# An S5, attention and DeltaNet kernel on one core: whole-row rotations in S5, one sum moved to GpSimd, small copies moved to ScalarE

## The chip, the cores and the metric

The kernel runs on one core of one Trainium2 chip. Its time is the device time of one execution in microseconds; three runs of the kernel before gave 1975.92, 1976.27 and 1977.36, median 1976.27. Besides, one execution was profiled, and all durations below come from that one.

## The reference

Two layers of a hybrid backbone run over 128 context tokens and 512 latent tokens, 640 in all, with 1024 features each. Layer 0 mixes with two heads side by side, layer 1 with a gated DeltaNet; a squared-ReLU MLP follows each, and every sub-layer has its norm and its modulation by a condition. The change lies in the mixer of layer 0:

```
def _s5_scan(u, lam_re, lam_im, log_dt, b_re, b_im, c_re, c_im, x0):
    lam_bar = jnp.exp(lam * jnp.exp(log_dt)[:, None])
    b_bar = ((lam_bar - 1) / lam)[..., None] * lax.complex(b_re, b_im)
    bu = jnp.einsum('gnp,blgp->blgn', b_bar, u)
    bu = bu.at[:, 0].add(lam_bar * x0)
    _, xs = lax.associative_scan(comb, (a, bu), axis=1)     # x_t = lam_bar x_(t-1) + bu_t, complex
    y = jnp.einsum('gpn,blgn->blgp', c_mat, xs).real
    return y, xs[:, -1]

def _even_mixer_latent(h, ck, cv, x0_re, x0_im, w_in, w_out, s5p, rpb):
    u, q, k, v = _even_split(h, w_in)
    a_out, _, _ = _s5_mixer(u, x0_re, x0_im, *s5p)          # forward and backward scan
    b_out = _neighbourhood_attention(q, k, v, ck, cv, rpb)  # 8 heads, windows of 8 x 16 and the cache
    return jnp.concatenate([a_out, b_out], axis=-1) @ w_out
```

S5 has 32 groups with 64 complex states each and two directions.

## The kernel before

All of layer 0 and 1 stays on the core; weights are streamed by SyncE's DMA queue. A weight block is loaded as fp32 (`raw`), split into a high part on ScalarE (`whi`, L194) and a low part on GpSimd (`wlo`, L196), and every product runs as three TensorE passes (L205 to L207).

The mixer of layer 0 first projects u, then q, k and v of four head pairs; between these products stand the steps of S5. S5 works in four blocks of eight groups, each with two directions `d`: eight units. Eight time steps are folded into one, so that a group has 65 folded steps of the latent stream and 17 of the context (82 columns; one of each holds the start state). A unit (`s5_unit`, L769) does this:

- VectorE builds the folded input weights `bp` (L785 to L787, two products and a sum of 1024 elements per partition). TensorE transposes them (L792) and multiplies them with the inputs (L809), and ScalarE copies the result to `W` (L811).
- VectorE builds the folded output weights `ct` (L798 to L800, two products and a sum of 1152 elements).
- The complex recurrence is turned into a real one: `W` is rotated by a table of angles, scanned with a real decay (L844, L846), and rotated back. Real and imaginary parts lie in partitions 0 to 63 and 64 to 127, so a rotation needs a swapped copy of its source: two DMAs on SyncE (L825, L826). Then `rotate` (L828) multiplies the source by the cosines (L832) and the swapped copy by the sines with its sign (L833), and adds them (L834).
- The final state is copied out (L851). A tile of start states goes into `W` by a copy of eight elements (L814).

`s5_tables` (L870) makes the cosines and sines of a block: GpSimd copies the first nine columns (L875), VectorE doubles them up to 65 (L864 to L867), and three DMAs bring them to the other halves of the partitions and to the other direction (L878, L879). The table has 65 columns; the 17 context columns use its first 17, so each product over 82 columns is two instructions, over 8 x 65 = 520 and over 8 x 17 = 136 elements.

`s5_taps` forms the taps (`kk`, L910, L912) from `ct`; `s5_back` multiplies states and inputs out (L938 to L942) and applies the gelu. Attention (`attention`, L966) runs in blocks of 128 queries: scores (L993), softmax, transposes of the probabilities (L1011), their copies from PSUM (`pT`, L1013 on ScalarE, L1015 on VectorE), products with the values (L1019). Beside it run the modulation products of later sub-layers (`mod_half`, L271), whose rows are copied from PSUM by VectorE (`mrow`, L287).

The order on every engine is set when the program is built: a planner with a cost model of its own places each instruction of the whole program, by priorities that the code gives; each engine then runs its list in that order. Tiles come from rings: `BUFS` (L1850) says how many buffers a tag has, and the writer of a buffer waits for the last reader of the tile that had it before.

Of the kernel before, what the change touches and what calls it, by code (L numbers as in the profile page):

```python
# [148 lines left out]
class Build:  # L149
# [94 lines left out]
    def mod_setup(self):  # L244
# [15 lines left out]
        self.raws = {}  # L260

# [9 lines left out]
    def mod_half(self, l, nb, kh, P, tag="pc", row=None, dst=None):  # L271
# [11 lines left out]
        if kh == 1:  # L283
            rp, rt, rb = row or (self.sp, "nf", 3)
            row = rp.tile([128, 256], F32, name="mrow", tag=rt, bufs=rb)
            if dst is None:
                nc.vector.tensor_copy(row, p[:, :256])  # L287
            else:
                nc.scalar.activation(row, p[:, :256], AF.Copy)
# [479 lines left out]
    def s5_unit(self, b, d, P, U, tb):  # L769
# [30 lines left out]
        V.tensor_tensor(ct, ct, t2, op=SU)  # L800
# [13 lines left out]
        V.tensor_copy(W[:, :, ex:ex + 1], self.s5x0[:, ps].unsqueeze(2))  # L814
        V.memset(W[:, :, ez:ez + 1], 0.0)

        def segs(t):
            so = t[:, :, 0:65], t[:, :, 65:82]
            return so
        def tab(t):  # L820
            return (t, t[:, :, 0:17]) if d == 0 else (t[:, :, ::-1], t[:, :, 16::-1])
# [6 lines left out]
        def rotate(src, op, out):  # L828
            sw = swap(src, "sw")
            m = self.tl([128, 8, 82], "s5g")  # L830
            for so, c_, s_, w_, m_ in zip(segs(src), tab(tb[:, 0]), tab(tb[:, 1]), segs(sw), segs(m)):
                V.tensor_tensor(m_, so, c_, op=M)  # L832
                V.scalar_tensor_tensor(w_, w_, sgn, s_, op0=M, op1=M)  # L833
            V.tensor_tensor(out, m, sw, op=op)  # L834
# [16 lines left out]
        V.tensor_copy(self.s5fin[:, p0:p0 + 8].unsqueeze(2), Sv[:, :, fin:fin + 1])  # L851
# [18 lines left out]
    def s5_tables(self, b, P):  # L870

        nc = self.nc
        t = [self.tl([128, 2, 8, 65], "rt") for d in range(2)]
        w = self.PA.tile([128, 512], F32, name="rt1")
        nc.gpsimd.tensor_copy(t[0][:, :, :, 0:9], self.s5e[:, :, 8 * b:8 * b + 8])  # L875
        self.turns(t[0], 8, 64, w)
        for r in range(2):
            nc.sync.dma_start(out=t[1][64 * r:64 * r + 64], in_=t[0][64:128])  # L878
        nc.sync.dma_start(out=t[0][64:128], in_=t[0][0:64])  # L879
# [86 lines left out]
    def attention(self, hp, qkv, ab, P):  # L966
# [16 lines left out]
        def block(qs, keys, vts, kind):  # L983
# [24 lines left out]
            for hh in range(2):  # L1008
# [3 lines left out]
                if hp < 2 or hh:  # L1012
                    nc.scalar.activation(pT[hh][:, :n], p[:, :n], AF.Copy)  # L1013
                else:
                    V.tensor_copy(pT[hh][:, :n], p[:, :n])  # L1015
# [834 lines left out]
    BUFS = dict(s5g=6, s5s=6, s5o=3, bp=1, bpt=1, ct=4, rt=2, vts=2,  # L1850
                cv=3, khT=2, ktok=2, vtok=2, cb=2, otok=2, osq=1)

    def run(self, stop=None):
        nc, A, tc = self.nc, self.A, self.tc
        with contextlib.ExitStack() as es:
# [35 lines left out]
            with contextlib.ExitStack() as ph:  # L1891
# [11 lines left out]
                with phase("l0") as P:  # L1903
# [5 lines left out]
                    steps, qkv = self.even_s5(hn, P)  # L1909
                    rx.close()  # L1910
# [17 lines left out]
                    for m in mods:  # L1928
                        self.mod_half(*m, P, tag="pb")
                    with tc.high_priority(offset=1000):  # L1930
# [67 lines left out]
```

## Time and profile before

| | us |
|---|---|
| median of three runs | 1976.27 |
| the profiled execution | 1976.35 |
| its span, first to last instruction | 1974.1 |
| TensorE busy | 1799.6 (91%) |
| VectorE busy | 1290.8 (65%) |
| ScalarE busy | 869.5 (44%) |
| GpSimd busy | 760.8 (39%) |

The profile's page gives shares over the whole span; the parts of the program have different limits, so the views below are cut to stretches. Times in a trace are counted from the first instruction. The letters PE, PEld, DVE, ACT, POOL and SPq stand for TensorE's matmuls, its weight loads, VectorE, ScalarE, GpSimd and SyncE's issues. A busy matmul time is a modelled one, since matmuls overlap.

### The profile page before, as it was taken

Reading aid. Unit: us, or ns where it says so; the run is one execution under the profiler, and the core shown is the slowest. Engines: PE = TensorE matmul, PEld = TensorE weight load, DVE = VectorE, ACT = ScalarE, POOL = GpSimd, SP = SyncE. Lnnn points to the kernel's source line nnn. Section 1 sums busy time; section 2 is a strip of 40 time slices with the busy share of each in tenths; the row PEclk is TensorE's granted clock in tenths of the full one; section 3 lists DMA queues with packets and bytes.
Section 4 is the critical chain, followed back from the end, with each engine's and each line's share of the span. In section 5 each row is a group of like instructions: output and inputs, shape, how many; then the busy total and the mean of one; then the engine's idle time right before and its main releaser. Section 6 shows DMA issues by size and latency. Waiting matters only on the chain. (4 is left out here: it accounts for less than half of the span.)

```text
span 1974.1 us, 35755 instructions
## 1 busy us (share of the span) xinstructions
PE 1799.6 (91%) x13556; PEld 1698.3 (86%) x13556; DVE 1290.8 (65%) x2825; ACT 869.5 (44%) x1928; POOL 760.8 (39%) x609
## 2 busy tenths in 40 slices
PE   5889889998999999998877889889989899999998
PEld 3789677988999999998877788787878899999997
DVE  8999777369264544548589988774667927364553
ACT  4333356344244353536454455344324425344362
POOL 2622101442343433453455555522235334343451
PEclk9999999998999999998998999898989999999999
DMA  8446886524332222332576478758834122222231
GB/s 319 131 112 169 239 246 228 195 106 140 124 112 84 76 86 75 135 123 78 158 207 196 117 197 238 222 166 267 279 131 149 54 97 76 86 76 86 76 96 54
DMA packets 206985, 286.61 MB, mean 145 GB/s; under 512 B 54879, under 2 KB 138237, under 8 KB 206813
## 3 DMA queue, kind: packets, MB, share of 16 engines
q1 hardware_dynamic: 206812, 284.33, 45.6%
q8 instruction: 107, 1.75, 0.4%
q14 instruction: 66, 0.53, 0.1%
HBM read 228.87 MB, written 46.82 MB: 140 GB/s over the span
## 5 line engine op out<-in xcount | busy, mean ns | idle before, releaser
L196 POOL TENSOR_TENSOR wlo<-raw,whi 128x1024 fp32r<-128x1024 f32 (+1 forms) x153 | 360.8, 2361 | 512.6 <-ACT whi L194 466.6
L194 ACT ACTIVATE whi<-raw 128x1024 fp32r<-128x1024 f32 (+1 forms) x153 | 153.2, 1002 | 324.5 <-PE pg L206 146.6
L207 PE MATMUL pg<-hidh,wlo 128*128 128x320 f32 (+2 forms) x576 | 178.8, 311 | 0.5 <-POOL wlo L196 0.5
L205 PE MATMUL pg<-hidh,whi 128*128 128x320 f32 (+2 forms) x576 | 179.0, 311 | 0.0
L206 PE MATMUL pg<-hidl,whi 128*128 128x320 f32 (+2 forms) x576 | 178.9, 311 | 0.0
L205 PE MATMUL pg<-h10h,whi 128*128 128x320 f32 x472 | 158.9, 337 | 17.5 <-DVE cb L1722 6.5
L422 DVE SCALAR_TENSOR_TENSOR x<-pg,mod,x 128x128 f32<-128x128 f32 (+2 forms) x132 | 53.7, 436 | 179.5 <-PE pg L207 179.5
L206 PE MATMUL pg<-h10l,whi 128*128 128x320 f32 x472 | 155.9, 330 | 0.0
L207 PE MATMUL pg<-h10h,wlo 128*128 128x320 f32 x472 | 155.3, 329 | 0.0
L205 PE MATMUL pa<-hidh,whi 128*128 128x320 f32 x448 | 138.0, 310 | 0.5 <-ACT whi L194 0.5
L207 PE MATMUL pa<-hidh,wlo 128*128 128x320 f32 x448 | 138.4, 309 | 0.0
L206 PE MATMUL pa<-hidl,whi 128*128 128x320 f32 x448 | 138.2, 309 | 0.0
L422 DVE SCALAR_TENSOR_TENSOR x<-pa,mod,x 128x128 f32<-128x128 f32 (+2 forms) x108 | 43.8, 435 | 136.8 <-PE pa L207 136.8
L507 POOL TENSOR_TENSOR wq<-S,wq 128x512 fp32r<-128x512 f32 x52 | 71.3, 1371 | 114.4 <-ACT wq L506 114.4
L205 PEld LDWEIGHTS pg<-h10h,whi 128*128 128x128 f32 x472 | 95.9, 203 | 21.4 <-DVE cb L1722 7.2
L207 PEld LDWEIGHTS pg<-hidh,wlo 128*128 128x128 f32 x576 | 108.2, 188 | 1.6 <-POOL wlo L196 1.0
L205 PEld LDWEIGHTS pg<-hidh,whi 128*128 128x128 f32 x576 | 108.3, 188 | 0.9 <-issue 0.8
L206 PEld LDWEIGHTS pg<-hidl,whi 128*128 128x128 f32 x576 | 108.2, 188 | 0.4 <-DVE hidl L568 0.3
L1322 DVE SCALAR_TENSOR_TENSOR cv<-cb,cw,cv 128x642 f32<-128x642 f32 x90 | 94.6, 1052 | 9.8 <-ACT cv L1319 8.9
L206 PEld LDWEIGHTS pg<-h10l,whi 128*128 128x128 f32 x472 | 95.9, 203 | 0.6 <-issue 0.4
L207 PEld LDWEIGHTS pg<-h10h,wlo 128*128 128x128 f32 x472 | 95.6, 203 | 0.2
L205 PEld LDWEIGHTS pa<-hidh,whi 128*128 128x128 f32 x448 | 83.9, 188 | 2.0 <-ACT whi L194 1.2
(742 smaller groups left out, 5754.2 us busy)
## 6 DMA issues: line engine op xcount, KB each, us to landing
raw<-in_wff SPq DMA_DIRECT2D x104, 512.0 KB
mraw<-in_wmod SPq DMA_DIRECT2D x96, 512.0 KB
raw<-in_wino SPq DMA_DIRECT2D x33, 512.0 KB
rawx<-in_wff SPq DMA_DIRECT2D x24, 512.0 KB
raw<-in_wine SPq DMA_DIRECT2D x16, 512.0 KB
cka<-pd SPq DMA_DIRECT2D x28, 256.0 KB
ckb<-pd SPq DMA_DIRECT2D x28, 256.0 KB
s5g<-s5g SPq DMA_DIRECT2D x32, 164.0 KB
```

Source lines behind the costliest of these rows:

```text
L194: nc.scalar.activation(hi[:, :kt], raw[:, :kt], AF.Copy)
L196: (nc.vector if self.lov and self.nw % self.lov else nc.gpsimd).tensor_tensor(lo[:, :kt], raw[:, :kt], hi[:, :kt], op=ALU.subtract)
L205: nc.tensor.matmul(p[:, :n], hi[:, k], xh[:, s], start=(k == 0), stop=False)
L206: nc.tensor.matmul(p[:, :n], hi[:, k], xl[:, s], start=False, stop=False)
L207: nc.tensor.matmul(p[:, :n], lo[:, k], xh[:, s], start=False, stop=(k == kt - 1))
L422: nc.vector.scalar_tensor_tensor(x[m][:, s], p[:, ls], g, x[m][:, s], op0=ALU.mult, op1=ALU.add)
L507: (V if j % 2 else nc.gpsimd).tensor_tensor(t[:, 4:8], src, t[:, 0:4], op=SU)
L1322: V.scalar_tensor_tensor(cv, cb[m][:, t:t + 642], cw[:, t:t + 1], cv, op0=M, op1=AD)
```

## The change

Five edits in the mixer of layer 0. The tables of angles get 82 columns (17 of them copies, made by GpSimd), so that `rotate` needs one instruction per product; the first product now overwrites its source, and the tile `m` goes, with one buffer of the ring `s5g`. The sum that ends `ct` goes from VectorE to GpSimd. The copies of start and final states, of all `pT`, and of `mrow` while the mixer runs go from VectorE to ScalarE.

```
@@ mod_half
-            if dst is None:
+            if dst is None and not self.rowact:
                 nc.vector.tensor_copy(row, p[:, :256])
             else:
                 nc.scalar.activation(row, p[:, :256], AF.Copy)
@@ s5_unit
-        V.tensor_tensor(ct, ct, t2, op=SU)
+        nc.gpsimd.tensor_tensor(ct, ct, t2, op=SU)
...
-        V.tensor_copy(W[:, :, ex:ex + 1], self.s5x0[:, ps].unsqueeze(2))
+        nc.scalar.activation(W[:, :, ex:ex + 1], self.s5x0[:, ps].unsqueeze(2), AF.Copy)
...
-        def segs(t):
-            so = t[:, :, 0:65], t[:, :, 65:82]
-            return so
-        def tab(t):
-            return (t, t[:, :, 0:17]) if d == 0 else (t[:, :, ::-1], t[:, :, 16::-1])
+        tc_, ts_ = (tb[:, n] if d == 0 else tb[:, n, :, ::-1] for n in range(2))
...
             sw = swap(src, "sw")
-            m = self.tl([128, 8, 82], "s5g")
-            for so, c_, s_, w_, m_ in zip(segs(src), tab(tb[:, 0]), tab(tb[:, 1]), segs(sw), segs(m)):
-                V.tensor_tensor(m_, so, c_, op=M)
-                V.scalar_tensor_tensor(w_, w_, sgn, s_, op0=M, op1=M)
-            V.tensor_tensor(out, m, sw, op=op)
+            V.tensor_tensor(src, src, tc_, op=M)
+            V.scalar_tensor_tensor(sw, sw, sgn, ts_, op0=M, op1=M)
+            V.tensor_tensor(out, src, sw, op=op)
...
-        V.tensor_copy(self.s5fin[:, p0:p0 + 8].unsqueeze(2), Sv[:, :, fin:fin + 1])
+        nc.scalar.activation(self.s5fin[:, p0:p0 + 8].unsqueeze(2), Sv[:, :, fin:fin + 1], AF.Copy)
@@ s5_tables
-        t = [self.tl([128, 2, 8, 65], "rt") for d in range(2)]
+        t = [self.tl([128, 2, 8, 82], "rt") for d in range(2)]
...
-        self.turns(t[0], 8, 64, w)
+        self.turns(t[0][:, :, :, 0:65], 8, 64, w)
         for r in range(2):
-            nc.sync.dma_start(out=t[1][64 * r:64 * r + 64], in_=t[0][64:128])
-        nc.sync.dma_start(out=t[0][64:128], in_=t[0][0:64])
+            nc.sync.dma_start(out=t[1][64 * r:64 * r + 64, :, :, 17:82], in_=t[0][64:128, :, :, 0:65])
+        nc.sync.dma_start(out=t[0][64:128, :, :, 0:65], in_=t[0][0:64, :, :, 0:65])
+        nc.gpsimd.tensor_copy(t[0][:, :, :, 65:82], t[0][:, :, :, 0:17])
+        nc.gpsimd.tensor_copy(t[1][:, :, :, 0:17], t[1][:, :, :, 17:34])
@@ attention
-                if hp < 2 or hh:
-                    nc.scalar.activation(pT[hh][:, :n], p[:, :n], AF.Copy)
-                else:
-                    V.tensor_copy(pT[hh][:, :n], p[:, :n])
+                nc.scalar.activation(pT[hh][:, :n], p[:, :n], AF.Copy)
@@ BUFS
-    BUFS = dict(s5g=6, s5s=6, s5o=3, bp=1, bpt=1, ct=4, rt=2, vts=2,
+    BUFS = dict(s5g=5, s5s=6, s5o=3, bp=1, bpt=1, ct=4, rt=2, vts=2,
```

The planner makes a new order from this, here at three places. First SyncE, where attention's first loads stand. `s5g<-s5g` is a swap of S5, `kT`, `qz` and `vt` are the keys, queries and values of the first head pair, `mraw` a modulation weight. Before:

```order
L825 DMA s5g<-s5g 64x656
L826 DMA s5g<-s5g 64x656
L268 DMA mraw<-in_wmod 128x1024
L1112 DMA qkv_2334<-qs 128x640
L825 DMA s5g<-s5g 64x656
L826 DMA s5g<-s5g 64x656
L974 DMA kT<-qkv_1321 128x640
L976 DMA qz_2569<-qkv_1383 64x640
L976 DMA qz_2570<-qkv_1383 64x640
L977 DMA vt<-qkv_1487 128x1024
```

And in the changed program, in its own line numbers (L822 and L823 are the swap, L972 to L975 the loads of keys, queries and values):

```order
L1107 DMA qkv_2189<-qs 128x640
L822 DMA s5g<-s5g 64x656
L823 DMA s5g<-s5g 64x656
L1107 DMA qkv_2310<-qs 128x640
L875 DMA rt<-rt 64x16x65
L269 DMA mraw<-in_wmod 128x1024
L972 DMA kT<-qkv_1311 128x640
L974 DMA qz_2539<-qkv_1373 64x640
L974 DMA qz_2540<-qkv_1373 64x640
L975 DMA vt<-qkv_1479 128x1024
L979 DMA nab<-in_nab 128x512 x2
```

The swap between the last store of a q or k tile and the load of `kT` has moved behind the loads.

Second GpSimd, from the first table copy (`rt<-s5e`) on; `wlo` are the low parts of projection weights, `s5o` a cleared margin. Before:

```order
L875 COPY rt<-s5e 128x16x9
L196 TENSOR_TENSOR wlo<-raw,whi 128x1024 x3
L931 MEMSET s5o 128x8
L196 TENSOR_TENSOR wlo<-raw,whi 128x1024
L875 COPY rt<-s5e 128x16x9
L196 TENSOR_TENSOR wlo<-raw,whi 128x1024 x3
L875 COPY rt<-s5e 128x16x9
```

Changed, with the sum of `ct` (L801) and the copies of 17 columns (L876, L877) among them:

```order
L871 COPY rt<-s5e 128x16x9
L196 TENSOR_TENSOR wlo<-raw,whi 128x1024 x2
L801 TENSOR_TENSOR ct<-ct,s5tmp 128x1152
L196 TENSOR_TENSOR wlo<-raw,whi 128x1024
L801 TENSOR_TENSOR ct<-ct,s5tmp 128x1152
L877 COPY rt<-rt 128x16x17
L876 COPY rt<-rt 128x16x17
L929 MEMSET s5o 128x8
L196 TENSOR_TENSOR wlo<-raw,whi 128x1024
L801 TENSOR_TENSOR ct<-ct,s5tmp 128x1152
L871 COPY rt<-s5e 128x16x9
L196 TENSOR_TENSOR wlo<-raw,whi 128x1024 x2
```

Three sums and two copies have come between the low parts in the first block.

Third VectorE, at the third sum of `bp` in the program (`bp<-bp,s5tmp`) and the first rotation (L832, L833 before; L827, L828 in the changed program). Before:

```order
L786 TENSOR_TENSOR s5tmp<-pwi,Bb_924 128x8x128
L785 TENSOR_TENSOR bp<-pwr,Bb_923 128x1024
L832 TENSOR_TENSOR s5g<-s5g,rt 128x8x65
L833 SCALAR_TENSOR_TENSOR s5g<-s5g,cst,rt 128x8x65
L832 TENSOR_TENSOR s5g<-s5g,rt 128x8x17
L833 SCALAR_TENSOR_TENSOR s5g<-s5g,cst,rt 128x8x17
L787 TENSOR_TENSOR bp<-bp,s5tmp 128x1024
L834 TENSOR_TENSOR s5g<-s5g 128x656
```

Changed:

```order
L786 TENSOR_TENSOR bp<-pwr,Bb_923 128x1024
L787 TENSOR_TENSOR s5tmp<-pwi,Bb_924 128x8x128
L788 TENSOR_TENSOR bp<-bp,s5tmp 128x1024
L827 TENSOR_TENSOR s5g<-s5g,rt 128x656
L828 SCALAR_TENSOR_TENSOR s5g<-s5g,cst,rt 128x656
L800 TENSOR_TENSOR s5tmp<-pwi,s5bc_757 128x1152
L829 TENSOR_TENSOR s5g<-s5g 128x656
```

The third sum of `bp` has come ahead of the rotation, and the rotation is one product and one signed product of 656 elements.

## Rows read from the trace of the kernel before

**Rows 1.** Busy time by stretch: from:to us, length, then each engine's busy us.
```profile
84.00:209.00 125.00, 108.18 (x799) 104.56 (x798) 111.74 (x167) 46.94 (x91) 35.10 (x19) 0.96 0.56 152
209.00:360.00 151.00, 131.24 (x1143) 104.89 (x1141) 116.82 (x265) 78.97 (x228) 13.82 (x13) 0.97 0.73 225
900.00:1500.00 600.00, 521.28 (x4470) 489.06 (x4469) 447.05 (x1009) 278.21 (x618) 278.04 (x301) 0.92 0.64 190
```

**Rows 2.** TensorE's waits in 84 to 360 us: total us, times, longest.
```profile
PE pb L792 <- DVE bp L787: 9.8, 2, 5.3
PE pa L993 <- DMA qz<-qkv: 5.4, 1, 5.4
...
PE pb L792 <- DVE kk L910: 2.0, 1, 2.0
PE pa L993 <- DVE mtmp L294: 1.8, 1, 1.8
PE pa L291 <- DVE mrow L287: 1.7, 1, 1.7
PE pb L938 <- DVE kk L910: 1.7, 1, 1.7
```

**Rows 3.** Timeline before attention: start us, us, engine, line, [idle before it, and its releaser].
```profile
202.87 0.39 SPq L1112 DMA_DIRECT2D qkv<-qs  x1
208.74 1.53 DVE L844 TENSOR_TENSOR_SCAN s5g<-s5g 128x656 f32<-128x656 f32 x1
212.13 1.10 SPq L976 DMA_DIRECT2D qz<-qkv  x2
215.79 0.77 PE L993 MATMUL pa<-kT,qz 128*128 128x128 f32 x2 [5.45 <-DMA qz<-qkv]
```

**Rows 4.** VectorE by line, 84 to 360 us: count | busy us, mean ns | idle before.
```profile
L833 DVE SCALAR_TENSOR_TENSOR s5g<-s5g,cst,rt 128x520 f32<-128x520 f32 x16 | 14.3, 891 | 13.3 <-DMA s5g<-s5g 13.3
...
L800 DVE TENSOR_TENSOR ct<-ct,s5tmp 128x1152 f32<-128x1152 f32 x8 | 12.8, 1603 | 0.0
...
L832 DVE TENSOR_TENSOR s5g<-s5g,rt 128x520 f32<-128x520 f32 x16 | 11.1, 696 | 7.0 <-DMA rt<-rt 6.9
...
L832 DVE TENSOR_TENSOR s5g<-s5g,rt 128x136 f32<-128x136 f32 x16 | 6.8, 427 | 0.0
...
L834 DVE TENSOR_TENSOR s5g<-s5g 128x656 f32<-128x656 f32 x8 | 6.7, 832 | 0.1
...
L833 DVE SCALAR_TENSOR_TENSOR s5g<-s5g,cst,rt 128x136 f32<-128x136 f32 x16 | 5.6, 353 | 0.0
...
L1015 DVE COPY pT<-pg 128x384 f32<-128x384 f32 x8 | 4.4, 549 | 0.7 <-PE pc L1019 0.7
L287 DVE COPY mrow<-pa 128x256 f32<-128x256 f32 x10 | 4.2, 417 | 0.8 <-PE pa L281 0.8
...
L851 DVE COPY s5fin<-s5s 128x8 f32<-128x8 f32 x8 | 1.3, 158 | 0.0
```

**Rows 5.** VectorE's waits, 84 to 360 us: total us, times, longest.
```profile
DVE s5g L833 <- DMA s5g<-s5g: 13.3, 8, 2.7
```

**Rows 6.** Timeline: a table copy on GpSimd and the sum beside it.
```profile
130.98 0.84 DVE L834 TENSOR_TENSOR s5s<-s5g 128x656 f32<-128x656 f32 x1
131.01 0.98 POOL L875 COPY rt<-s5e 128x144 f32<-128x144 f32 x1 [7.77 <-DVE s5g L833]
```

**Rows 7.** Timeline: the sum of `ct`, alone and beside GpSimd.
```profile
102.56 1.34 DVE L800 TENSOR_TENSOR ct<-ct,s5tmp 128x1152 f32<-128x1152 f32 x1
...
109.76 3.35 POOL L196 TENSOR_TENSOR wlo<-raw,whi 128x1024 fp32r<-128x1024 f32 x1 [14.70 <-ACT whi L194]
...
110.90 3.42 DVE L800 TENSOR_TENSOR ct<-ct,s5tmp 128x1152 f32<-128x1152 f32 x1
```

**Rows 8.** Timeline of TensorE: the fourth group of transposes.
```profile
145.03 0.41 PE L792 MATMUL pb<-cst,bp 128*128 128x128 f32 x2 [4.41 <-DVE bp L787]
```

**Rows 9.** ScalarE by line, 84 to 360 us.
```profile
L908 ACT ACTIVATE kk<-pb 128x256 f32<-128x256 f32 x4 | 1.5, 379 | 2.3 <-PE pb L905 2.3
```

More of the change, by code (lines that the diff above doesn't have):

```diff
@@ L260, in mod_setup @@
         self.raws = {}
+        self.rowact = False
     def mod_load(self, l, nb, kh, P, tag=None):
@@ L872, in s5_tables @@
         nc = self.nc
-        t = [self.tl([128, 2, 8, 65], "rt") for d in range(2)]
-        w = self.PA.tile([128, 512], F32, name="rt1")
+        t = [self.tl([128, 2, 8, 82], "rt") for d in range(2)]
+        w = P.tile([128, 512], F32, name="rt1")
         nc.gpsimd.tensor_copy(t[0][:, :, :, 0:9], self.s5e[:, :, 8 * b:8 * b + 8])
-        self.turns(t[0], 8, 64, w)
+        self.turns(t[0][:, :, :, 0:65], 8, 64, w)
         for r in range(2):
-            nc.sync.dma_start(out=t[1][64 * r:64 * r + 64], in_=t[0][64:128])
-        nc.sync.dma_start(out=t[0][64:128], in_=t[0][0:64])
+            nc.sync.dma_start(out=t[1][64 * r:64 * r + 64, :, :, 17:82], in_=t[0][64:128, :, :, 0:65])
+        nc.sync.dma_start(out=t[0][64:128, :, :, 0:65], in_=t[0][0:64, :, :, 0:65])
+        nc.gpsimd.tensor_copy(t[0][:, :, :, 65:82], t[0][:, :, :, 0:17])
+        nc.gpsimd.tensor_copy(t[1][:, :, :, 0:17], t[1][:, :, :, 17:34])
         return t
@@ L1909, in run @@
                     steps, qkv = self.even_s5(hn, P)
+                    self.rowact = True
                     rx.close()
@@ L1929, in run @@
                         self.mod_half(*m, P, tag="pb")
+                    self.rowact = False
                     with tc.high_priority(offset=1000):
```

## The prediction

> **What bounds the kernel now.** I read the busy times by stage first [rows 1]. TensorE is busy 521.3 of 600 us in the DeltaNet layer and 87% of each of the two stages that the change edits: 84 to 209 us, in which the q, k, v projections and the first S5 blocks run together, and 209 to 360 us, attention with the rest of S5. In the first of these VectorE is busy 111.7 of 125 us, in the second 116.8 of 151. So TensorE sets the end and stands still when something is late. The reader is to see in [rows 1] that the two edited stages hold only 16.8 + 19.8 = 36.6 us of TensorE idle: no edit here can win more than that, and what is saved on VectorE counts only where TensorE waits for it.
>
> The waits of TensorE in 84 to 360 us [rows 2] say where. 9.8 us go to the transposes of S5's input weights (`bp`), 2.0 and 1.7 us to the taps' sum (`kk`), 1.8 and 1.7 us to the modulation rows (`mtmp`, `mrow`): 17.0 us on VectorE. 5.4 us go to the loads of the first head pair's queries. Then I followed the 5.4 us back to its issuer [rows 3]. SyncE had issued the last store of q and k at 202.87 us and next stood before a swap that needs the result of the scan that began at 208.74 us and took 1.53; the loads of `kT` and `qz` were queued behind that swap, those of `qz` went out at 212.13 us, and TensorE took up attention at 215.79 us.
>
> **The change part by part.**
>
> *Rotations.* A rotation had two products over 520 and two over 136 elements, and one sum [rows 4]. Per element the rows give (832 - 696) / 136 = 1.0 ns, so 696 ns holds a fixed part of about 0.17 us. One product over 656 elements instead of two saves one fixed part; two products per rotation and 16 rotations give 32 x 0.17 = 5.4 us of VectorE. By the rows' means it would be up to 16 x (0.70 + 0.43 + 0.89 + 0.35 - 2 x 0.83) = 11 us, but 427 and 891 ns are means that a few stalls lengthen. I take 5.
>
> The merged product overwrites its source, so it must wait until the swap has read it. Before, the product over 520 elements could run while the swap was under way, and only the second product waited: 13.3 us in 8 times [rows 5]. If nothing else is put there, the first product moves behind the wait: at most 8 x 0.83 = 6.6 us more of S5's chain, at least nothing, since the order has other sums there. The tables' copies of 17 columns also come between a transfer and a rotation that already waited 6.9 us for it [rows 4]. A copy of 144 elements took 0.98 us with its wait [rows 6]; that is up to 4 us for the four blocks. I take 1 us for both on the path: the order shows other VectorE work ahead of most rotations, and 11 us is the far end.
>
> *The last sum on GpSimd.* It frees VectorE of eight sums [rows 4] of 1.34 us undisturbed [rows 7], 10.7 us. But [rows 7] also show what a GpSimd sum does to VectorE: the same sum took 3.42 us when GpSimd began one of 1024 elements at 109.76 us, 2.08 us more. In proportion, a sum of 1152 elements would hold VectorE for 2.08 x 1152 / 1024 = 2.3 us. Six of the eight stand in the first stage, by the order ahead of the `qz` clears. There: 6 x (2.3 - 1.34) = +5.8 us. Five table copies stand there too; the copy in [rows 6] ended 0.17 us after the sum beside it on VectorE, which for 272 elements gives 0.17 x 272 / 144 = 0.3 us each, +1.5. Against that stand 11 of the 16 rotations, 11 x 0.34 = -3.7 us, and eleven copies of eight elements (`L814`, `L851`) at the 158 ns of [rows 4], -1.7 us. VectorE's work in the first stage thus changes by +1.9 us: the sum's move eats what the rotations give. If GpSimd always found VectorE idle it would be -8.0 - 3.7 - 1.7 = -13.4 us. What reaches TensorE I put at zero: the order sets the fourth group of `bp` transposes, the one that waited 4.4 us [rows 8], and the taps nine and more matmuls later on TensorE, and the `bp` sum earlier among VectorE's rows. The bounds are -5 us (half of the 9.8) and +8 us.
>
> *Small copies to ScalarE.* Off VectorE go ten `pT` copies (4.4 us for eight), twelve `mrow` (4.2 us for ten) and sixteen of eight elements [rows 4], together some 12 us, nearly all in the second stage. ScalarE takes a PSUM block of 256 elements in 379 ns [rows 9], so some 9 us go to an engine that is busy 79.0 of 151 us [rows 1]. TensorE waited 3.5 us for the chain through `mrow` [rows 2]; a copy on ScalarE is no longer behind a sum of 1.3 us on VectorE. I take -2 us; ends are -3.5 and, when ScalarE's exponentials get in front, +3.
>
> *What the new order moves.* This is the largest term and the change's text does not name it. In the changed program SyncE issues `kT` and `qz` of the first head pair right after the last-but-one stores, the third table transfer and a weight load, and the swap of the scan's result stands 16 issues later. Without that wait the loads go out soon after 203 us. From issue to use took 215.79 - 212.13 = 3.7 us [rows 3], so they land near 208 us, ahead of 215.79 - 5.4 = 210.4 us, when TensorE had finished what stood before attention. The 5.4 us go. Late next is that very swap: it now stands behind the loads of two head pairs, 16 issues of about 0.6 us (two `qz` issues took 1.10 us), so it goes out near 213 us instead of 210.3, which S5's chain feels. I take -4 us, ends -5.4 and 0.
>
> *The DeltaNet layer.* No line of it changes, yet its order does, on all engines, since the order is planned for the whole program. TensorE idles 78.7 us there [rows 1]. No row says which order is better; I take 0, and a tenth of that idle time, 8 us, each way.
>
> The sum: 0 (first stage) + 1 (rotations' waits) - 2 (copies) - 4 (loads) + 0 = -5 us. The profiled execution took 1976.35 us, its span 1974.1; it lies 0.08 us above the median of 1976.27 of the runs, so no correction is needed. Forecast: 1971 us.
>
> **The rivals.**
>
> *GpSimd's sums hold VectorE up (slower).* The place is block 1 of S5 in the first stage, where VectorE has 13 us to spare in 125. For it speaks [rows 7]; against it, that GpSimd's sums can fall where VectorE waits for a swap anyway. Price: all of the +1.9 us, 1.5 us again for copies that wait out a sum, 6.6 us for products moved behind their swaps, nothing from `mrow`, and half the loads' gain lost because the swap is late: 1.9 + 1.5 + 6.6 - 2 = +8, 1984 us. It decides from the point where the fourth `bp` sum ends later against TensorE's row than before. The Trainium skill, "SBUF — State Buffer", section "SBUF: two separate sides", says that VectorE and GpSimd share one pair of ports under an exclusive lock, held for a whole instruction, when VectorE reads two inputs from SBUF and GpSimd reads SBUF as well. By that rule each of the eight sums costs VectorE more than it frees, and none shares. The trace agrees for the 2.08 us above; for the 0.98 us copy the sum on VectorE beside it took its usual 0.84 us [rows 6], so there GpSimd was the one that waited.
>
> *No change.* The loads of `qz` wait for something else: GpSimd clears half of each `qz` tile, and that clear now stands behind table copies which wait for transfers; or the memory, freed by the projections' last reads, comes free at the same time. Then -4 becomes 0, and the rest, -1, cannot be told from nothing: 1975 us.
>
> *More than forecast.* TensorE's waits for `bp` fall by half, the swap's delay is hidden, all of `mrow`'s wait goes: -5 - 5.4 - 3.5 + 1 = -13, 1963 us. For it speaks that VectorE's own rows before the fourth `bp` sum become fewer; against, the 111.7 us of 125.
>
> **How the numbers follow.** Less than 0.2% (4 us) cannot be told from no change. Forecast, with its own range of 1967 to 1975: 0.40, three quarters of it faster. No change: 0.20. More than forecast: 0.14. Slower by GpSimd's sums: 0.26. The DeltaNet layer's new order blurs each: of no change a quarter goes to either side. Faster: 0.30 + 0.14 + 0.05 = 0.49; same: 0.10 + 0.10 + 0.05 = 0.25, the last from the weaker part of the slower case; slower: 0.05 + 0.21 = 0.26. The range for 8 in 10 reaches from more than forecast less half of the DeltaNet layer's 8 us, 1959, to the slower case and half of its 8 us more, 1988.
>
> **What would show it.** Right: at the start of attention TensorE waits under 1 us for `qz`; the merged products take about 0.83 us; the eight `ct` sums stand on GpSimd with VectorE rows of over 3 us beside them; TensorE's waits for `mrow` are under 1 us; VectorE's busy time in 84 to 209 us within 5 us of before. Wrong: a wait for `bp` or `kk` that grows beyond 13.5 us in all; a new wait of TensorE for `wlo` behind a GpSimd row that waits for a table; the wait for `qz` still there; or a difference that lies after 900 us, where no line changed.

## The result, and the profile after

The changed kernel takes 1992.85 us (median of 7 runs, 1984.68 to 1999.35) where the kernel before takes 1976.54 beside it: 1.0080 times as long, 95% interval 1.0058 to 1.0102, or +15.8 us (11.5 to 20.2). The forecast was 1971 us, its range ended at 1988. In what follows a time "against before" is the ratio to the kernel before on the same chip less one, times 1977 us; a run's interval is about 3 us each way (4.4 for the changed kernel), so the difference of two is uncertain by some 4.5 us.

The residual sums of `x` begin when the first layer's mixer ends; by their first and last start the two traces can be laid on each other (count, shortest, median and longest ns, first and last start). Of the kernel before:

```profile
L422 DVE SCALAR_TENSOR_TENSOR x<-pg,mod,x x132: 335/408/553, 363.6 to 1854.4; 128x128 f32<-128x128 f32 x44, 128x192 f32<-128x192 f32 x44, 128x320 f32<-128x320 f32 x44
```

Of the changed kernel:

```profile
L423 DVE SCALAR_TENSOR_TENSOR x<-pg,mod,x x132: 339/409/552, 380.6 to 1871.3; 128x128 f32<-128x128 f32 x44, 128x192 f32<-128x192 f32 x44, 128x320 f32<-128x320 f32 x44
```

The first stands 17.0 us later, the last 16.9. In these two executions all of the loss lies in the mixer of the first layer, none in the DeltaNet layer, whose order also moved. The busy times of the kernel before from 84 us to its mixer's end (columns as in [rows 1]; the last three are the granted clock, the DMA share and GB/s):

```profile
84.00:363.60 279.60, 243.02 (x1953) 213.05 (x1952) 228.56 (x431) 125.91 (x318) 48.92 (x32) 0.96 0.66 194
```

And of the changed kernel, with the first stretch of [rows 1] and one short stretch besides:

```profile
84.00:209.00 125.00, 100.63 (x734) 98.19 (x734) 105.89 (x123) 41.00 (x84) 52.91 (x24) 0.92 0.47 124
138.90:145.70 6.80, 2.70 (x13) 2.70 (x14) 6.80 (x15) 2.00 (x6) 2.50 (x1) 0.50 0.28 104
84.00:380.60 296.60, 250.28 (x1952) 218.14 (x1952) 221.98 (x353) 135.52 (x354) 79.17 (x48) 0.93 0.63 182
```

VectorE does less (222.0 us instead of 228.6) and the layer takes 17 us more: it is not VectorE's work that grew. TensorE stands idle for 46.3 us instead of 36.6, and the same matmuls (1953 and 1952 records) take 7.3 us longer, at a mean granted clock of 0.93 instead of 0.96: 9.7 + 7.3 = 17.0 us. The second part comes after waits. TensorE stood idle from 135.1 to 143.0 us, for instance, and from 138.9 to 145.7 us the granted clock was 0.50, the lower of its two levels (1.2 and 2.4 GHz). By the trace's clock records it stood at that level for 41.0 us of this stretch, and for 23.7 us in the kernel before. What TensorE waits for, 84 to 380.6 us:

```profile
PE pg L205 <- ACT qs L1085: 8.3, 3, 3.9
PE pb L793 <- DVE kk L908: 7.9, 1, 7.9
PE pb L793 <- DVE bp L788: 5.4, 1, 5.4
PE pa L991 <- DMA qz<-qkv: 5.0, 1, 5.0
PE pc L1100 <- ACT qs L1085: 3.6, 2, 3.1
...
PE pb L936 <- DVE kk L908: 1.4, 1, 1.4
...
PE pa L292 <- ACT mrow L290: 0.5, 1, 0.5
```

Against [rows 2], `bp` costs 5.4 instead of 9.8 us and `mrow` 0.5 instead of 1.7, but the taps' sum `kk` 9.3 instead of 3.7, and the wait for `qz` is still there. The largest growth is that of `qs`, ScalarE's copies of the projections q, k and v out of PSUM: 8.3 + 3.6 = 11.9 us, where the kernel before has 1.0:

```profile
PE pc L1105 <- ACT qs L1090: 1.0, 2, 0.8
```

Of these waits, that for `kk` and one for `qs` stand behind S5 in another engine's list. The taps come from `ct`, but their sum follows on VectorE after rows of S5, and the first of these, a product that overwrites its source, waited 4.87 us for the swap. On ScalarE a `qs` copy followed the copy of a final state, one of the small copies that the change put there, and that one waited 9.02 us for S5's sum. The longest wait for `qs`, 3.9 us, came from another side: ahead of that copy ScalarE splits weights, and waited 8.33 us for their load; why the load was late was not followed.

```profile
135.55 0.84 DVE L827 TENSOR_TENSOR s5g<-s5g,rt 128x656 f32<-128x656 f32 x1 [4.87 <-DMA s5g<-s5g]
...
142.77 0.18 DVE L908 TENSOR_TENSOR kk<-pb,kk 128x32 f32<-128x32 f32 x1
```

```profile
171.56 1.06 ACT L194 ACTIVATE whi<-raw 128x1024 fp32r<-128x1024 f32 x1 [8.33 <-DMA raw<-in_wine]
...
206.24 0.21 ACT L846 ACTIVATE s5fin<-s5s 128x8 f32<-128x8 f32 x1 [9.02 <-DVE s5s L829]
206.36 0.67 ACT L1085 ACTIVATE qs<-pg 128x128 f32<-128x128 f32 x2
```

So TensorE feels a late S5 through the lists of the other engines, and it feels it ahead of attention. The last `qs` copy starts at 224.2 instead of 206.8 us (before, then changed), and attention at 231.81 instead of the 215.79 of [rows 3], so that 16.0 of the 17.0 us are lost by then:

```profile
L1090 ACT ACTIVATE qs<-pg x33: 258/555/845, 86.0 to 206.8; 128x128 f32<-128x128 f32 x11, 128x192 f32<-128x192 f32 x11, 128x320 f32<-128x320 f32 x11
```

```profile
L1085 ACT ACTIVATE qs<-pg x33: 255/538/830, 85.8 to 224.2; 128x128 f32<-128x128 f32 x11, 128x192 f32<-128x192 f32 x11, 128x320 f32<-128x320 f32 x11
```

```profile
231.81 0.77 PE L991 MATMUL pa<-kT,qz 128*128 128x128 f32 x2 [4.96 <-DMA qz<-qkv]
```

S5 is serial over four blocks: a block's tables are laid into the tiles that the block before must have read for the last time. The backward scans (first and last start) of the kernel before and of the changed one:

```profile
L846 DVE TENSOR_TENSOR_SCAN s5g<-s5g x4: 1511/1518/1524, 137.3 to 276.4; 128x656 f32<-128x656 f32 x4
```

```profile
L841 DVE TENSOR_TENSOR_SCAN s5g<-s5g x4: 1518/1522/4202, 145.0 to 312.6; 128x656 f32<-128x656 f32 x4
```

S5 is 7.7 us late in its first block and 36.2 us in its last, and the mixer ends 17.0 us late: what S5 lost behind the start of attention cost the layer 1 us. The longest new part of the chain is the way of the tables, from the last turn over three transfers to the first rotation. In block 1 of the kernel before (timeline; SPq is SyncE's queue):

```profile
149.32 0.41 DVE L867 TENSOR_TENSOR rt<-rt,rt 128x256 f32<-128x256 f32 x1
149.79 1.17 SPq L878 DMA_DIRECT2D rt<-rt  x2
...
154.13 0.46 SPq L879 DMA_DIRECT2D rt<-rt  x1
...
157.76 0.70 DVE L832 TENSOR_TENSOR s5g<-s5g,rt 128x520 f32<-128x520 f32 x1 [1.76 <-DMA rt<-rt]
```

In block 1 of the changed kernel:

```profile
155.98 2.88 DVE L862 TENSOR_TENSOR rt<-rt,rt 128x256 f32<-128x256 f32 x1
158.88 1.38 SPq L874 DMA_DIRECT2D rt<-rt  x2
...
164.80 0.41 SPq L193 DMA_DIRECT2D raw<-in_wine  x1
165.31 0.83 SPq L875 DMA_DIRECT2D rt<-rt  x1
...
172.57 0.42 POOL L876 COPY rt<-rt 128x272 f32<-128x272 f32 x1 [7.06 <-DMA rt<-rt]
173.03 2.99 DVE L827 TENSOR_TENSOR s5g<-s5g,rt 128x656 f32<-128x656 f32 x1 [6.29 <-POOL rt L876]
```

The third transfer overwrites what the first two read, so it goes out when these have landed: after 6.4 us instead of 4.3. From its issue to the next row it is 7.3 us (3.6 before); that row is now the copy. Not all of this is the transfer itself. The planner has put a weight load (`raw`) ahead of it, which before stood behind it, and by the trace's packet records the third transfer's first packet follows 3.7 us after its issue (1.1 before), while its packets take 2.8 us (2.1 before). From the pair's issue to the rotation it is 14.2 us instead of 8.0; over the four blocks 12.5, 14.2, 13.9 and 17.9 us, 58.5 in all, instead of 7.6, 8.0, 9.2 and 8.7, 33.5 in all. These 25 us are the larger part of S5's 36. The pages' DMA rows, of the kernel before and of the changed one, show what changed in the transfers:

```profile
DMA packets 206985, 286.61 MB, mean 145 GB/s; under 512 B 54879, under 2 KB 138237, under 8 KB 206813
```

```profile
DMA packets 218504, 286.61 MB, mean 144 GB/s; under 512 B 67166, under 2 KB 150524, under 8 KB 218332
```

The same bytes, 11519 packets more. A table of 65 columns fills its tile, and a transfer moves 64 unbroken stretches of 1040 elements. In a tile of 82 columns the 65 lie in 16 rows with gaps, and each transfer is 64 x 16 pieces of 260 bytes: 12 transfers x 64 x 15 = 11520 packets more.

The second new part is on GpSimd. VectorE's waits that answer to [rows 5], and its and GpSimd's rows by line (84 to 330 us) that answer to [rows 4]:

```profile
DVE s5g L827 <- DMA s5g<-s5g: 14.0, 5, 4.9
DVE s5g L827 <- POOL rt L876: 12.7, 4, 6.3
```

```profile
L828 DVE SCALAR_TENSOR_TENSOR s5g<-s5g,cst,rt 128x656 f32<-128x656 f32 x16 | 18.5, 1157 | 0.0
L827 DVE TENSOR_TENSOR s5g<-s5g,rt 128x656 f32<-128x656 f32 x16 | 17.9, 1118 | 27.8 <-DMA s5g<-s5g 14.0 <-POOL rt L876 12.7 <-DMA out_nv<-vts 1.1
...
L801 POOL TENSOR_TENSOR ct<-ct,s5tmp 128x1152 f32<-128x1152 f32 x8 | 25.5, 3188 | 48.0 <-DVE ct L799 27.4 <-DVE s5tmp L800 19.3 <-DVE s5g L816 1.3
```

The products are one instruction each, but their mean is 1.14 us where an undisturbed one takes 0.84: single rows beside GpSimd take 2 us more. The plainest is a scan in the middle of the chain, 3.82 instead of 1.52 us:

```profile
126.09 3.18 POOL L801 TENSOR_TENSOR ct<-ct,s5tmp 128x1152 f32<-128x1152 f32 x1 [2.86 <-DVE s5tmp L800]
126.84 3.82 DVE L839 TENSOR_TENSOR_SCAN s5g<-s5g 128x656 f32<-128x656 f32 x1
```

### The profile page after: what moved, and what is told of

Same layout as the page of the kernel before. It is cut to its first block, busy times and chain, and to the rows that moved or that the text cites. A ratio compares the mean times of both kernels' runs of the same rounds, so it can differ in the third digit from the quotient of the medians.

```text
span 1991.1 us, 35759 instructions
## 1 busy us (share of the span) xinstructions
PE 1803.1 (91%) x13556; PEld 1698.5 (85%) x13556; DVE 1284.5 (65%) x2747; ACT 877.9 (44%) x1966; POOL 791.4 (40%) x625
## 4 chain that ended last, share of the span: by engine, by line
PE 25%; DVE 13%; DMA 8%; issue 2%; POOL 2%; SPq 2%; ACT 1%; POOLq 0%; DVEq 0%; ACTq 0%
PE pg L206 3%; PE pg L207 3%; PE pg L205 3%; DVE cv L1317 2%; DVE sbt L1420 2%; PE pa L207 2%; PE pa L206 2%; PE pa L205 2%; DVE ub L1422 2%; DMA gbb<-gbd 1%; PE pg L527 1%; PE pg L528 1%; PE pg L526 1%; PE pb L527 1%; PE pa L527 1%
## 5 line engine op out<-in xcount | busy, mean ns | idle before, releaser
L423 DVE SCALAR_TENSOR_TENSOR x<-pg,mod,x 128x128 f32<-128x128 f32 (+2 forms) x132 | 53.8, 436 | 172.4 <-PE pg L207 172.3
L423 DVE SCALAR_TENSOR_TENSOR x<-pa,mod,x 128x128 f32<-128x128 f32 (+2 forms) x108 | 43.9, 436 | 136.0 <-PE pa L207 136.0
L205 PEld LDWEIGHTS pg<-h10h,whi 128*128 128x128 f32 x472 | 94.2, 200 | 13.4 <-ACT cb L1309 8.9
```

What stands on the lines that cost most here:

```text
L205: nc.tensor.matmul(p[:, :n], hi[:, k], xh[:, s], start=(k == 0), stop=False)
L423: nc.vector.scalar_tensor_tensor(x[m][:, s], p[:, ls], g, x[m][:, s], op0=ALU.mult, op1=ALU.add)
```

## The experiments

Three theories were tested: T, the tables' transfers in pieces; G, the sum on GpSimd; P, products that overwrite their source and so wait for the swap. Each run went beside the kernel before. The whole list, against before; the last column is the first residual sum of the run's one profiled execution, less the 363.6 us of the kernel before:

| run | what it has | ratio (95%) | us | mixer's end, us |
|---|---|---|---|---|
| changed | all three parts | 1.0080 (1.0058-1.0102) | +15.8 | +17.0 |
| e1 | sum on VectorE again | 1.0016 (0.9999-1.0033) | +3.2 | +4.2 |
| e2 | whole-row transfers | 1.0034 (1.0014-1.0053) | +6.7 | +5.1 |
| e13 | first product in its own tile | 1.0056 (1.0042-1.0069) | +11.1 | +11.2 |
| e4 | small copies alone | 0.9955 (0.9939-0.9972) | -8.9 | -7.2 |
| e8 / e9 | S5's small copies / `mrow`, `pT` | 0.9971 (0.9954-0.9989) / 0.9954 (0.9940-0.9968) | -5.7 / -9.1 | -0.4 / -2.0 |
| e3 | e4 + sum on GpSimd | 1.0001 (0.9985-1.0016) | +0.2 | +3.6 |
| e7 | e4 + an idle GpSimd sum | 0.9997 (0.9984-1.0009) | -0.6 | +5.7 |
| e6 | e4 + tables in pieces | 1.0014 (0.9998-1.0031) | +2.8 | +1.1 |
| e14 | e4 + overwriting | 0.9966 (0.9949-0.9984) | -6.7 | -6.0 |
| e12 | e4 + half a table by ScalarE | 0.9978 (0.9965-0.9992) | -4.3 | -2.3 |
| e5 | e1 + whole rows | 1.0028 (1.0015-1.0041) | +5.5 | +8.5 |
| e10 | e5, 17-column copies on ScalarE | 1.0015 (1.0002-1.0029) | +3.0 | +3.9 |
| e11 | e10 + own tile | 0.9966 (0.9950-0.9981) | -6.7 | -2.4 |
| e15 | e11 + pieces | 1.0051 (1.0033-1.0068) | +10.1 | +11.0 |
| e16 | e11 + sum on GpSimd | 1.0007 (0.9993-1.0022) | +1.4 | +2.6 |

Every edit gives the planner a new order for the whole program. Behind the mixer, where no edit stands, the profiled executions differ too: from the first residual sum to the last of L422 (L423 in most runs) they take 1482.5 (e8) to 1497.1 us (e10), and 1490.8 in the kernel before. So a time against before can hold some 8 us that don't come from the mixer; whether they come from the new order or from that one execution is not shown. A price is told with more trust where pairs of kernels agree in both columns.

**The small copies (e4, e8, e9).** e4 is the kernel before with the edits of `mrow`, `pT` and S5's copies of eight elements; e8 has the last two lines alone, e9 the rest alone.

```diff
-            if dst is None:
+            if dst is None and not self.rowact:
...
-                if hp < 2 or hh:
-                    nc.scalar.activation(pT[hh][:, :n], p[:, :n], AF.Copy)
-                else:
-                    V.tensor_copy(pT[hh][:, :n], p[:, :n])
+                nc.scalar.activation(pT[hh][:, :n], p[:, :n], AF.Copy)
...
+        nc.scalar.activation(W[:, :, ex:ex + 1], self.s5x0[:, ps].unsqueeze(2), AF.Copy)
+        nc.scalar.activation(self.s5fin[:, p0:p0 + 8].unsqueeze(2), Sv[:, :, fin:fin + 1], AF.Copy)
```

> Only the third part: the small copies on ScalarE, all else as before. My prediction priced it at -2 us (ends -3.5 and +3): 1974. Theories T, G and P all say no slower than before; were it slower by more than 4 us, the small copies on ScalarE would be a cause of their own.

> The kernel before with only the sixteen copies of eight elements (S5's start and last state) on ScalarE; mrow and pT stay as before. My prediction put the gain of all small copies down to TensorE's waits for mrow. If that is so: no change here, within 3 us of before. Rival E: the copies of eight elements stood behind GpSimd's sums in S5's chain (one of them took 2.37 us, one 1.88 instead of 0.16), and they are what the small copies won: 5 to 9 us under before.

> The kernel before with only the copies of mrow and pT on ScalarE; S5's copies of eight elements stay on VectorE. All small copies gave -8.7 us, those of eight elements -5.6. If the two add: -3 us. My prediction's reason (TensorE waited 3.5 us for the chain through mrow): -2 to -3.5. If it is S5's copies alone: 0.

The small copies win 8.9 us, four times their price, and 7.2 us of it show in the mixer. Each half wins by itself, 5.7 and 9.1 us, but in their profiled executions the mixer ends only 0.4 and 2.0 us earlier. That the halves add up, or do not, is not shown, nor where most of their gains come from. In e4 TensorE waits 6.2 us for `bp` and 2.5 for `qz` (9.8 and 5.4 in [rows 2]), and its idle time falls from 36.6 to 26.6 us:

```profile
PE pb L793 <- DVE bp L788: 6.2, 2, 5.4
...
PE pa L995 <- DMA qz<-qkv: 2.5, 1, 2.5
```

**The sum on GpSimd (e1, e3, e7, e16).** e1, e3 and e16 move one line one way or the other. In e7 the line stays on VectorE, and behind it stands `nc.gpsimd.tensor_tensor(t2, ct, ct, op=SU)`, one more sum that nobody reads, into the scratch tile that the products of the next unit need. The edit of e1:

```diff
-        nc.gpsimd.tensor_tensor(ct, ct, t2, op=SU)
+        V.tensor_tensor(ct, ct, t2, op=SU)
```

> The changed kernel with the last sum of the output weights back on VectorE; tables, rotations and small copies as changed. In the changed kernel S5's last scan result is 34.5 us later than before (330.9 against 296.4) and the end of the layer 17 us later, so about 17 us of S5's delay are hidden. Theory T (tables: the transfers in pieces of 65 elements and the copies behind them lengthen the way from the last turn to the first rotation from 7.6-9.2 us to 12.5-17.2 us per block, 25 us in all): most of S5's delay stays, about 25 us, the kernel is 8 us slower than before, near 1985. Theory G (GpSimd's sums stretch VectorE's rows by 2 us each, and that is what S5 loses): S5's delay falls to under 10 us, the time to 1974-1978. Theory P (the products that overwrite their source wait for the swap): no change against the changed kernel, 1990-1993.

> Only two of the three parts: the sum on GpSimd and the small copies on ScalarE; tables of 65 columns, rotations in two products and their own tile as before. Theory T: S5 keeps its times of before within 10 us, 1972-1978. Theory G: slower than before by most of the 16 us, 1985-1992. Theory P: as T, 1972-1978, since the products no longer overwrite their source; T and P are told apart by the whole-row transfers.

> The small copies alone (the sum stays on VectorE), and behind each sum GpSimd does one more sum of the same 1152 elements into the scratch tile, which nothing reads. Theory G (a GpSimd sum stretches VectorE's row beside it and holds the scratch tile): as with the sum on GpSimd, 6 to 11 us above the small copies alone, -3 to +2 us against before, with eight VectorE rows lengthened by about 2 us. Rival L (the sum on GpSimd costs because the output weights come later to TensorE): as the small copies alone, -9 us, within 3.

> As the run with own tile and whole rows (-6.7 us against before), but the sum on GpSimd. Theory G: 8 us more, as in both other pairs: 0 to +4 against before. If the sum costs only where S5 waits for tables or swaps anyway: -7 to -3.

e4 to e3 costs 9.1 us, e11 to e16 8.1, e1 to the changed kernel 12.6; only e5 to e2, where e5 lost time in another way (below), costs 1.2. By the mixer's end it is 10.8, 5.0 and 12.8 us, and 3.4 won from e5 to e2. e4 to e7 costs 8.3 us, though there VectorE keeps its sum: GpSimd's rows beside VectorE and their hold on the scratch tile are enough for a loss of this size. Theory G holds. Rival L, the output weights that come later, is not ruled out as the way in which it acts: in e7 the third sum of `ct` starts at 130.0 us, in e4 at 124.6, so the weights are late there too. Beside e7's idle sums:

```profile
116.61 2.96 POOL L802 TENSOR_TENSOR s5tmp<-ct 128x1152 f32<-128x1152 f32 x1 [2.75 <-DVE ct L801]
...
118.07 2.05 DVE L834 TENSOR_TENSOR s5g<-s5g,rt 128x520 f32<-128x520 f32 x1 [0.47 <-DMA rt<-rt]
```

The product took 2.05 us instead of 0.70; in block 1 the tables of e7 went out at 156.8 us, in e4 at 148.8.

**The tables in pieces (e2, e6, e15).** e2 fills the forward gap before the transfers and sends one stretch per partition. e6 does the opposite to e4: tiles of 66 columns of which 65 are used, so that the transfers break, and nothing else in the text. e15 breaks e11's, and needs one more copy of 17 columns on ScalarE behind the third transfer.

```diff
+        self.turns(t[0][:, :, :, 0:17], 8, 16, w)
+        nc.gpsimd.tensor_copy(t[0][:, :, :, 65:82], t[0][:, :, :, 0:17])
+        self.turns(t[0][:, :, :, 0:65], 16, 64, w)
+        f0, f1 = (x.rearrange("p a b c -> p (a b c)") for x in t)
...
-            nc.sync.dma_start(out=t[1][64 * r:64 * r + 64, :, :, 17:82], in_=t[0][64:128, :, :, 0:65])
-        nc.sync.dma_start(out=t[0][64:128, :, :, 0:65], in_=t[0][0:64, :, :, 0:65])
+            nc.sync.dma_start(out=f1[64 * r:64 * r + 64, 17:1312], in_=f0[64:128, 0:1295])
+        nc.sync.dma_start(out=f0[64:128], in_=f0[0:64])
```

```diff
-        t = [self.tl([128, 2, 8, 65], "rt") for d in range(2)]
+        t = [self.tl([128, 2, 8, 66], "rt")[:, :, :, 0:65] for d in range(2)]
```

> The changed kernel with the tables sent as whole rows: the last 17 columns of the first table are filled right after the first turn, before the transfers, and the three transfers move one unbroken stretch per partition; the sum stays on GpSimd, the rotations stay merged. Theory T: from the last turn to the first rotation of a block 8-10 us again, S5's delay about 10 us, which the layer hides: 1974-1979. Theory G: the tables' way gets shorter but VectorE's stretched rows stay, 1985-1992. Theory P: 1988-1993.

> The small copies alone, and the tables laid in rows of 66 columns of which 65 are used, so that the transfers move pieces of 65 elements; no merged product, no copy of 17 columns. Theory T by its transfers: from the pair's issue to the third transfer's about 6.5 us instead of 4.4, from the third to the first rotation about 5 instead of 3.6; 3.5 us per block, S5 some 14 us late in all, the time 4 to 10 us above the small copies alone, so -5 to +1 us against before. If it is the copies of 17 columns behind the transfers or the merged products: as the small copies alone, -9 us.

> As the run with own tile and whole rows (-6.7 us against before), but the tables sent in pieces of 65 elements and the forward table's upper 17 columns copied behind the third transfer, on ScalarE. Theory T: the pieces cost here what they cost beside the small copies alone, about 11 us: +2 to +7 against before. If the merged products make up for it: -7 to -2.

e6 costs 11.7 us over e4 (8.3 by the mixer's end), as much as the whole rotation edit (e4 to e1: 12.1 and 11.4). Block 1 of e6 shows the changed kernel's way without a merged product or a GpSimd copy in it, 13.2 us where e4 needs 8.4 (148.85 to 157.26):

```profile
150.95 1.38 SPq L880 DMA_DIRECT2D rt<-rt  x2
...
157.53 0.65 SPq L881 DMA_DIRECT2D rt<-rt  x1
...
164.16 0.70 DVE L833 TENSOR_TENSOR s5g<-s5g,rt 128x520 f32<-128x520 f32 x1 [5.00 <-DMA rt<-rt]
```

Over the four blocks it is 57 us against 33 in e4, and S5's last scan starts at 296.5 instead of 268.7 us. e11 to e15 costs 16.8 us (13.4), and whole rows in the changed kernel (e2) win 9.1 (11.9): theory T holds. What costs is the pieces with the order that the planner makes for them. In e6 too the weight load stands ahead of block 1's third transfer (issued at 156.98 us), in e4 behind it, and no run has the pieces without this. The Trainium skill, "DMA: Bandwidth & Descriptors", section "Why small descriptors are slow (HBM only)", says that transfers between SBUF and SBUF do not suffer from small pieces. These do: by the packet records the pair of block 1 has landed 5.7 us after its issue in e6, 4.0 in e4, with no weight load between, and the measurement decides.

**Overwriting the source (e5, e10, e11, e13, e14).** e5 is e1 with whole rows, e10 has both 17-column copies on ScalarE besides. e11 and e13 give the first product its own tile again, in e10 and in the changed kernel; e14 takes it away from e4.

```diff
+            m = self.tl([128, 8, 82], "s5g")
-            V.tensor_tensor(src, src, tc_, op=M)
+            V.tensor_tensor(m, src, tc_, op=M)
...
-            V.tensor_tensor(out, src, sw, op=op)
+            V.tensor_tensor(out, m, sw, op=op)
```

> The changed kernel with both repairs: tables sent as whole rows, the sum on VectorE; merged products and small copies as changed. So far, against before: sum back -> +3 us, whole rows -> +7, old rotations -> -1, small copies alone -> -9. Theory T (what the rotation edit costs is the tables' way alone): with whole rows the edit costs nothing, so this run lies within 3 us of the small copies alone, 6 to 12 us under before. Theory P (the products that overwrite their source and the five instead of six S5 tiles cost too): 0 to 5 us under before, and S5's waits for swaps grow.

> Whole rows, the sum on VectorE, merged products and small copies as changed, as in the run that came out at +6 against before; there the first copy of 17 columns on GpSimd stood 10.3 us beside VectorE's rows and the first scan came 9.8 us late. Now both copies of 17 columns are on ScalarE. Theory T' (the rotation edit costs by its tables alone: pieces, and copies that wait on GpSimd): the first scan near 123 us again, the time near the small copies alone, -5 to -10 us against before. Theory P (products that overwrite their source, and five S5 tiles instead of six): S5's delay grows block by block as before, 0 to +5 us.

> As the run with both copies of 17 columns on ScalarE, but the first product of a rotation goes into a tile of its own instead of over its source, from the same ring of five S5 tiles. If the overwriting costs (theory P), this is 2 to 6 us faster than that run; if it doesn't, the same within 3 us, or slower by up to 5 us because the ring of five runs short.

> The changed kernel with one thing undone: the first product of a rotation goes into a tile of its own (from the ring of five) and no longer over its source. Transfers in pieces, copies of 17 columns on GpSimd and the sum on GpSimd stay. Theory P+T, not additive (pieces alone or overwriting alone give the rotation edit's whole 12 us): little is won, 8 to 16 us above before. Theory P (overwriting is the main cause in this kernel): about 10 us won, +3 to +8 against before.

> The small copies alone, and both products of a rotation written over their source; tables of 65 columns in unbroken transfers, two products, six S5 tiles as before. Theory P: overwriting by itself costs about 10 us, so +1 us against before (-2 to +4). If overwriting only costs with the new tables or with five tiles: as the small copies alone, -9 us (-12 to -6).

Overwriting costs 9.7 us between e11 and e10 (6.3 by the mixer's end), 4.7 in the changed kernel (e13, within its uncertainty of zero; 5.8), 2.2 in e14, also within it (1.2); e15 has its own tile and is 6.9 us slower than e1, which overwrites. So it costs with whole rows, and no price that holds in every kernel is shown. In e13 TensorE's wait for `kk` behind the product is down to 1.9 us, but `qs` and `qz` cost 7.5 and 7.4. What overwriting can do is seen in e10. After a scan of block 2 the two products stand behind the mixer's rows, and 21.7 us pass between the scan's start and the sum of the rotation:

```profile
218.58 1.52 DVE L839 TENSOR_TENSOR_SCAN s5g<-s5g 128x656 f32<-128x656 f32 x1
...
233.89 0.84 DVE L827 TENSOR_TENSOR s5g<-s5g,rt 128x656 f32<-128x656 f32 x1
...
240.27 0.83 DVE L829 TENSOR_TENSOR s5s<-s5g 128x656 f32<-128x656 f32 x1
```

In e11 the product needs no swap, stands right behind the scan, and the sum follows 8.0 us after the scan's start:

```profile
207.39 1.52 DVE L840 TENSOR_TENSOR_SCAN s5g<-s5g 128x656 f32<-128x656 f32 x1
208.95 0.84 DVE L828 TENSOR_TENSOR s5g<-s5g,rt 128x656 f32<-128x656 f32 x1
...
215.38 0.83 DVE L830 TENSOR_TENSOR s5s<-s5g 128x656 f32<-128x656 f32 x1
```

Whole rows and overwriting together won nothing (e1 to e10, 0.2 us; e1 to e5, none), although the pieces were gone. In e10 the place above is where part of it went; whether it is the overwriting or the order that the program happened to get there is not settled. In e5 a GpSimd copy ahead of the transfers, shown at the end, made the first scan 6 us later than in e1 (133.0 against 126.9 us). The other parts of the rotation edit are cheap together: e11 has the merged products, the ring of five tiles and, which the text of the change does not name, the doublings' scratch tile in another pool, and it lies 2.2 us behind e4, within the uncertainty.

**A shorter way of the tables (e12).** One of the three transfers of e4 becomes a ScalarE copy.

```diff
-        for r in range(2):
-            nc.sync.dma_start(out=t[1][64 * r:64 * r + 64], in_=t[0][64:128])
+        nc.sync.dma_start(out=t[1][0:64], in_=t[0][64:128])
+        nc.scalar.activation(t[1][64:128], t[0][64:128], AF.Copy)
```

> The small copies alone, and of the three table transfers per block one is replaced: the upper half of the backward table is copied by ScalarE (same partitions, 1040 elements), the lower half stays a transfer. The transfers' way is on S5's chain (theory T): one transfer less before the third, 0.5 us less issue and at most 1 us less wait per block; if that carries through, 1 to 4 us under the small copies alone, -10 to -12 against before. If ScalarE's copy of about 1.2 us waits behind other work there: as the small copies alone or up to 4 us above, -9 to -5.

The tables' way became shorter (7.0, 6.6, 8.6 and 8.0 us, 30 instead of 33 in all), the kernel 4.6 us slower than e4, at the edge of what can be told: a miss. S5's last scan came at 275.9 us, 7 later than in e4, so what the transfers gave was lost elsewhere. The fastest kernels of this study are e4 and e9; none with a merged rotation was faster.

**Against the expectations.** e7, e8, e10, e13, e14 and e16 came where a theory had put them. e1 and e2 fell between T's and G's ranges, since both causes are at work. e3 alone looked as if the sum were free, until e4 showed what the small copies win. e4 and e9 won more than anybody expected, e5 fitted no range, and e6, e11 and e15 went the expected way but beyond the range.

## Why the prediction was wrong, point by point

The +15.8 us divide by way of measured kernels: small copies -8.9, the rotation edit +12.1 (e4 to e1), the sum +12.6 (e1 to the changed kernel). They add up because they are steps of one way; by the other way (e4, e3, changed) the sum is 9.1 and the rotation edit 15.6. The prediction had -2 for the copies, 0 for the first stage with the rotations' products and the sum in it, +1 for the rotations' waits and -4 for the loads.

*Rotations: the step that failed.* "I take 1 us for both on the path" priced the overwriting and the 17-column copies and left out a third thing, the transfers' shape. VectorE is busy 6.6 us less in the layer, and it bought nothing. The tables' transfers went from 64 stretches to 1024 pieces each, the way of the tables grew by 25 us over four blocks, and e6 shows that the pieces, with the order made for them, are enough for the edit's price. The wait of the overwriting product, which the order was trusted to hide, is there as well: 4.87 us ahead of `kk`. The measured 12.1 us lie near the bound of 11 by luck, since the bound was made of other terms.

*The sum on GpSimd: the second failed step.* "What reaches TensorE I put at zero" came from a balance of VectorE's busy time. The rival had the cause. Its 8 us agree with the sum's price by luck: they were the price of the whole change, and 6.6 of them stood for the products behind their swaps. The sum and its stand-in in e7 cost 8.1 to 9.1 us in three pairs, the sum 12.6 in the changed kernel and 1.2 beside e5. Its place was not the fourth `bp` sum (5.4 us of waits instead of 9.8): it is S5's chain, where a stretched product, scan or turn delays what follows, and from there the lists of VectorE and ScalarE.

*The error behind both* is that busy time by stage was taken for the limit. S5 is a chain over four blocks with single tables, and its delay grew from block to block, of which the layer paid what came ahead of attention. The prediction never followed that chain from scan to scan, nor the rows of other engines that stand behind it, though [rows 4] showed its waits for tables. It had no term for the clock either: the longer matmul times after the waits make up 7.3 of the 17.0 us.

*Small copies:* right in sign, -8.9 instead of -2, beyond the bound of -3.5. The wait for `mrow` is gone as forecast (0.5 us), but that is 1.2 of the 8.9 us, so the reason given was not the main one; which is stays open. What the prediction left out is the price where S5 is late: the state's copy then holds up ScalarE's list (9.02 us above).

*The new order of SyncE:* the order was read rightly, and the term of -4 us failed by a time. The swap of the scan's result is no longer ahead of the loads, and these do go out right behind the last store, 2.5 us after it. But that store itself went out at 222.15 us instead of 202.87, since all of SyncE's list was late by then, and so the loads at 224.61, not near 203:

```profile
222.15 0.59 SPq L1107 DMA_DIRECT2D qkv<-qs  x1
222.84 0.63 SPq L875 DMA_DIRECT2D rt<-rt  x1
...
224.61 1.36 SPq L972 DMA_DIRECT2D kT<-qkv  x1
```

The prediction took the store's time from the kernel before.

*The DeltaNet layer:* right, 0; from the first residual sum to the last it is 1490.7 us against 1490.8. The bound of 8 us each way was needed for the other kernels (1482.5 to 1497.1), so the exact zero is in part luck.

*Signs named:* the undisturbed merged product takes 0.84 us and `mrow` waits 0.5, as said. VectorE's busy time in 84 to 209 us fell by 5.9 us, a little more than the 5 named. Of the signs against, `bp` and `kk` together reached 14.7 us (limit 13.5) and `qz` stayed at 5.0; these are the two that told.

## What to carry to other kernels

When a tile is widened, look at every transfer that reads or writes it: rows with gaps turn one stretch into as many pieces as rows, and the count of small packets on the page shows it. Where work is a chain over blocks, follow what an edit adds to each turn of it, and ask up to which turn the engine that sets the time feels it; busy time says nothing of this. Look also at what stands behind the chain's rows in the lists of the other engines. Measure the parts of a change one by one: here one part won 9 us, and the two others lost nearly three times as much.

## What the runs showed that was not expected

GpSimd can be the one that waits, and long. In e5 a copy of 272 elements, 0.42 us elsewhere, took 10.31 us while VectorE ran one two-input row after the other from 98.3 to 108.5 us:

```profile
98.55 10.31 POOL L873 COPY rt<-rt 128x272 f32<-128x272 f32 x1 [6.96 <-DVE rt L862]
```

The Trainium skill, "SBUF — State Buffer", section "SBUF: two separate sides", says that the loser of the shared ports blocks fully; the row agrees, and shows that it can lose several times in a row.
